# One place combination for split weights, and three changes of order, in a two-layer hybrid decoder trunk

## The chip, the cores and the metric

The kernel runs on one core of one Trainium2 chip. The metric is the device time of one execution in microseconds (us). Three runs of the kernel before took 598.81, 599.59 and 599.92 us, median 599.59. A difference of about 0.2% can be told from none.

## What is computed

Input and output are 256 tokens of width 1024 in float32. There are two layers, each a mixer and a feed-forward block, and a last norm:

```python
def rms_norm(x, g):
    return x * lax.rsqrt(jnp.mean(x * x, axis=-1, keepdims=True) + EPS) * g

def swiglu(h, w_gate, w_up, w_down):
    return (jax.nn.silu(h @ w_gate) * (h @ w_up)) @ w_down

# layer 0 mixer: RG-LRU (conv, gates, linear recurrence) beside stick-breaking attention
proj = h @ w_in;  out = concatenate([y_rg, y_sb]) @ w_out
# layer 1 mixer: S5 (diagonal complex state space model, gelu, GLU) beside block attention (MoBA)
proj = h @ w_in;  out = concatenate([y_s5, y_mb]) @ w_out

for layer in range(2):
    x = x + mixer(rms_norm(x, g_mix[layer]))
    x = x + swiglu(rms_norm(x, g_ffn[layer]), ...)
return rms_norm(x, final_norm)
```

The S5 branch has parameters of its own that come from few numbers: a step width exp(log_dt), from it a magnitude (tanh of xd/2 in the kernel) and a phase (sine of th), and from these powers and tables. They depend on no token.

## The kernel before

**Weights.** All dense weights lie in memory as 186 pieces of 128 x 1024 floats, in the order of their use. SyncE loads piece p into one of four buffers `raw`. ScalarE writes its rounded part `hi` (L109), VectorE the rest `lo` = raw - hi (L112). A product with float32 accuracy is then three TensorE matmuls: hi with the activations' high part, hi with their low part, lo with their high part (`dense` L152, `dense2` L163, the matmuls at L160 and L169; `proj_v` L352 with L368). A piece has eight blocks of 128 x 128 and so 24 such matmuls of 256 columns (in `proj_v` 12 of 512). `next_block` (L135) counts blocks. At the first block of piece p it has the piece p + 3 split and the piece p + 6 loaded; a load can land only where the piece four before it has been split.

**Places.** `split_tiles` (L102) takes the buffers of hi and lo out of one pool with five each, 1056 floats wide, and uses 1024 of them, from 0 or from 32 floats on, by a formula in p (L104). `half_line` reserves 16 floats between pools.

**Order.** TensorE and SyncE run in the order written. ScalarE, VectorE and GpSimd are put in order by the compiler's scheduler, from the written order and a model of times; `tc.issue_after(i)` makes the instructions of its block on i's own engine come behind i, and binds no other engine. Within an engine, order is fixed on the chip: an instruction that waits holds up all behind it.

**The norm.** x is split into xh and xl with the gain (`x_split` L219), unscaled by the token's 1/rms, which is multiplied in later. `x_square` (L210) squares x on ScalarE, two blocks at a time at the start, and GpSimd sums the squares (L215, L217). `rstd_a` (L237) sums over the partitions with TensorE (L241), takes a square root on ScalarE (L250; `preload_sqrt` at L202 loads its table early) and a chain of four small VectorE operations (L251 to L254). `rstd_b` (L257) spreads the result with TensorE (L260).

**Small operations in the background.** `s5_first` (L569) puts 38 VectorE operations of 128 x 16 on a list `bg`, the first part of the S5 parameters, down to xd (L606) and the clamped th (L612). `split_part` (L107) takes some from the list after each split: six up to piece 9, then two up to piece 40, then four. It is called before layer 0 begins (L1089).

**The start** (L1044 to L1089). x and pieces 0 and 1 are split in turns, then pieces 2 and 3, then all squares are taken behind piece 3's hi part. In `layer_ab` (L376), `softplus_setup` (L1022) does a Sigmoid on ScalarE, some 25 small GpSimd operations and a VectorE reciprocal (L1030) between them. The first `rstd_a` stands behind piece 4 in TensorE's order, `rstd_b` behind piece 5.

**S5 in the first feed-forward block.** `s5_prep` (L626) gives hooks that `ffn` (L273) calls. `early` (L801) comes after pair 0: `step0` (L646; Tanh L648, Sin L655 and L656, then small VectorE operations), `table` (L697; GpSimd products with `sq_phase` of VectorE between them), and GpSimd's larger work. All of it is told to issue after the norm's last sum (GpSimd) and after L254 (VectorE).

**The end of the second mixer** (`layer_cd` L815). `y_mm` (L896) computes a quarter of S5's output with 24 short matmuls, `y_gelu` (L905) takes it through four gelus on ScalarE. Quarters 0 and 1 come in the middle of `proj_v`, 2 and 3 behind it (L994, L995). Then come the four products of attention probabilities with v (`moba_av` L938; a copy to high part by ScalarE, L943, and low part by VectorE, L944), then four output columns of the projection that need only attention, then the S5 gate `dense(pg, yh, yl)`, which needs all quarters split (L1002, L1003).

Of the kernel before, what the change touches and what calls it, by code (L numbers as in the profile page):

```python
# [8 lines left out]
F32R = mybir.dt.float32r  # L9
AF = mybir.ActivationFunctionType  # L10
ALU = mybir.AluOpType
# [7 lines left out]
PI_F = 3.1415925  # L19
# [30 lines left out]
def trunk_kernel(  # L50
# [19 lines left out]
    def half_line(name, es=ctx, n=1):  # L70
        es.enter_context(tc.tile_pool(name="line_" + name, bufs=1)).tile([128, 16 * n], F32, name="line_" + name)
# [1 line left out]
    rawp = ctx.enter_context(tc.tile_pool(name="raw", bufs=LOAD_AHEAD - SPLIT_AHEAD + 1))  # L73
    half_line("a")
    wp = ctx.enter_context(tc.tile_pool(name="wp", bufs=SPLIT_AHEAD + 2))
    half_line("b", n=3)
    xp = ctx.enter_context(tc.tile_pool(name="xp", bufs=1))
    rp = ctx.enter_context(tc.tile_pool(name="rp", bufs=2))
    half_line("r")
# [5 lines left out]
    def nm(p):  # L85
        uid[0] += 1
        return f"{p}{uid[0]}"
# [13 lines left out]

    def split_tiles(p):  # L102
        if p not in hi:
            for d, n, o in ((hi, "hi", p // 6 + p % 5), (lo, "lo", p // 12 + p % 5 + 1)):  # L104
                d[p] = wp.tile([128, 1056], F32R, tag=n, name=nm(n))[:, 32 * (o % 2):32 * (o % 2) + 1024]

    def split_part(p, cs):  # L107
        split_tiles(p)
        last_hi[0] = S.activation(out=hi[p][:, cs], in_=raw[p][:, cs], func=AF.Copy)  # L109
        if pin:  # L110
            with tc.issue_after(pin[0].ins):
                i = V.tensor_sub(lo[p][:, cs], raw[p][:, cs], hi[p][:, cs])  # L112
        else:
            i = V.tensor_sub(lo[p][:, cs], raw[p][:, cs], hi[p][:, cs])
        with tc.issue_after(i.ins):
            for _ in range(min(BG if p > 40 else BG_AB if p < 10 else 2, len(bg))):
                bg.pop(0)()

    def split_half(p, c):
# [256 lines left out]
    def layer_ab():  # L376
# [128 lines left out]
        for j in range(2):  # L505
            ps = mmt()
            dense(ps[:, 0, :], xh, xl, ALL)
            if j == 0:
                y = rstd_a()
            dense(ps[:, 1, :], xh, xl, ALL)  # L510
            if j == 0:
                r = rstd_b(y)
                V.tensor_mul(xrp[:, 0, 3:T + 3], p2[0][:, 0, :], r)
                V.tensor_mul(xrp[:, 1, 3:T + 3], p2b, r)
                V.tensor_mul(xrp[:, 2:4, 3:T + 3], p2[1], bc(r, 2))
            V.tensor_mul(ti2[:, 2 * j:2 * j + 2, :], ps, bc(r, 2))
            conv(2 * j)
            conv(2 * j + 1)
# [50 lines left out]
    def s5_first():  # L569
# [8 lines left out]
        def ts(*a, **kw):  # L578
            ops.append(lambda: V.tensor_scalar(*a, **kw))
# [4 lines left out]
        def mul(*a):  # L584
            ops.append(lambda: V.tensor_mul(*a))
# [13 lines left out]
        for i in range(2):  # L599
# [3 lines left out]
            ts(out=g, in0=g, scalar1=127.0, scalar2=8388608.0, op0=ALU.add, op1=ALU.mult)  # L603
            ops.append(lambda: V.tensor_copy(out=gi, in_=g))
            mul(dt if i else p, p, gi.bitcast(F32))
        mul(xd, lr, dt)  # L606
        mul(th, li, dt)
        ts(out=k, in0=th, scalar1=1.0 / TWO_PI, scalar2=MAGIC, op0=ALU.mult, op1=ALU.add)
        ts(out=k, in0=k, scalar1=MAGIC, scalar2=None, op0=ALU.subtract)
        for c in (C1, C2, C3):  # L610
            stt(out=th, in0=k, scalar=-c, in1=th, op0=ALU.mult, op1=ALU.add)
        ts(out=th, in0=th, scalar1=PI_F, scalar2=-PI_F, op0=ALU.min, op1=ALU.max)  # L612
        bg.extend(ops)

    def s5_alloc():
# [10 lines left out]
    def s5_prep(es):  # L626
# [18 lines left out]

        def step0():  # L646
            xd, th, den, t = e16["xd"], e16["th"], e16["den"], t16("t")
            S.activation(out=t, in_=xd, func=AF.Tanh, scale=0.5)  # L648
            om, mag, em = t16("om"), t16("mag"), t16("em")
            V.tensor_scalar(out=om, in0=t, scalar1=-1.0, scalar2=1.0, op0=ALU.mult, op1=ALU.add)  # L650
# [164 lines left out]
    def layer_cd():  # L815
# [176 lines left out]
        pt[3] = moba_t(pr[3])  # L992
        ps1 = [mmt().rearrange("p a (b c) -> p (a b) c", c=64) for _ in range(2)]
        y_mm(ps1[0], 2)  # L994
        y_mm(ps1[1], 3)  # L995
        for h in range(4):
            moba_av(h, pt[h])
        y_gelu(ps1[0], 2)
        y_gelu(ps1[1], 3)
        for c in range(2):  # L1000
# [43 lines left out]
    with tc.manual_schedule(engines={mybir.EngineType.PE, mybir.EngineType.SP}):  # L1044
# [37 lines left out]
        x_split(4, 2, V_AB, lambda k: False)  # L1082
        split_half(1, 1)
        x_split(6, 2, V_AB, lambda k: False)
        split_to(3)
        with tc.issue_after(last_hi[0].ins):
            for k in range(0, 8, 2):
                x_square(k, 2)
        s5_first()  # L1089
        layer_ab()  # L1090
        s5_alloc()
        pes = ExitStack()
# [162 lines left out]
```

## Time and profile before

| | |
|---|---|
| median of 3 runs | 599.59 us |
| the profiled execution's own time | 598.55 us |
| its span, first to last instruction | 596.8 us |
| TensorE busy | 579.0 us, 97% |
| VectorE, ScalarE, GpSimd busy | 74%, 58%, 35% |
| mean granted TensorE clock | 0.994 |
| moved by DMA | 102.76 MB, mean 172 GB/s |

In the rows below, PE is TensorE, PEld its weight loads, DVE VectorE, ACT ScalarE, POOL GpSimd. L112 is line 112. Times are us from the span's start, unless ns. A timeline row gives start, duration, engine, line, operation, output<-inputs, shape and count, and in brackets the idle time before it with what ended it. Matmuls overlap and their ends are modelled, so the distance of two starts tells more than a duration.

### The profile page before, as it was taken

The numbers are of one execution on the slowest core, as the hardware profiler recorded it, in microseconds if no ns is written. First come the engines' busy times: TensorE is split into PE (matmuls) and PEld (weight loads), VectorE is DVE, ScalarE is ACT, GpSimd is POOL, SyncE is SP. The second block draws the span as 40 slices with busy tenths as digits, with TensorE's granted clock in tenths as the row PEclk, the third lists the DMA queues.
The fourth block names the chain that finished last, engine by engine and source line by source line (L and its number), as shares of the span: only waits on it lengthen the run. The fifth ranks groups of instructions, "written<-read, shape, count | busy, mean of one in ns | idle before, by whom it ended". The sixth has DMA issues, their size and how long they took to land.

```text
span 596.8 us, 11926 instructions
## 1 busy us (share of the span) xinstructions
PE 579.0 (97%) x4840; PEld 562.9 (94%) x4840; DVE 440.1 (74%) x636; ACT 346.2 (58%) x480; POOL 209.6 (35%) x203
## 2 busy tenths in 40 slices
PE   8899999999899999999999999999999999999994
PEld 7899889999799999999999998899999999999994
DVE  5798989896999986638966993688766665566632
ACT  6769996952345445464667268866645443445451
POOL 0810001538999999439920000013121110021131
PEclk9999999999999999999999999999999999999997
DMA  8755345653466676445544432264666666666601
GB/s 315 265 151 204 106 144 188 236 176 108 141 200 200 205 255 200 144 139 176 184 148 165 142 106 72 87 231 155 205 204 194 196 192 196 191 199 190 200 3 71
DMA packets 29319, 102.76 MB, mean 172 GB/s; under 512 B 3520, under 2 KB 3536, under 8 KB 29264
## 3 DMA queue, kind: packets, MB, share of 16 engines
q1 hardware_dynamic: 28080, 99.36, 51.0%
q10 hardware_dynamic: 864, 1.57, 0.7%
q0 software_dynamic: 320, 1.06, 0.5%
q8 instruction: 38, 0.62, 0.4%
q14 instruction: 17, 0.14, 0.1%
HBM read 100.93 MB, written 1.05 MB: 171 GB/s over the span
## 4 chain that ended last, share of the span: by engine, by line
PE 68%; DVE 13%; ACT 9%; issue 4%; POOL 3%; DMA 3%; SPq 0%; DVEq 0%; ACTq 0%; POOLq 0%
PE mm L160 59%; DVE lo L112 4%; PE mm L169 3%; ACT hi L109 2%; DMA raw<-wall 2%; ACT u L907 1%; DMA x<-xT 1%; PE ax L169 1%; PE ax L780 1%; POOL acc L217 1%; PE mm L903 1%; PE ax L852 1%; ACT s5tt L785 1%; POOL s5st L715 1%; POOL p_tmp L710 0%
## 5 line engine op out<-in xcount | busy, mean ns | idle before, releaser
L112 DVE TENSOR_TENSOR lo<-raw,hi 128x1024 fp32r<-128x1024 f32 x184 | 246.1, 1344 | 88.3 <-ACT hi L109 88.1
L109 ACT ACTIVATE hi<-raw 128x1024 fp32r<-128x1024 f32 (+1 forms) x188 | 195.3, 1048 | 166.5 <-PE mm L160 98.1
L160 PE MATMUL mm<-xh,hi 128*128 128x256 f32 x896 | 252.7, 282 | 0.8 <-ACT xh L943 0.7
L160 PE MATMUL mm<-xh,lo 128*128 128x256 f32 x896 | 248.8, 278 | 3.3 <-DVE lo L112 3.3
L160 PE MATMUL mm<-xl,hi 128*128 128x256 f32 x896 | 248.6, 277 | 0.2
L160 PEld LDWEIGHTS mm<-xh,lo 128*128 128x128 f32 x896 | 168.2, 188 | 4.4 <-DVE lo L112 4.3
L160 PEld LDWEIGHTS mm<-xh,hi 128*128 128x128 f32 x896 | 168.5, 188 | 1.8 <-ACT xh L943 1.2
L160 PEld LDWEIGHTS mm<-xl,hi 128*128 128x128 f32 x896 | 168.4, 188 | 0.9 <-DVE xl L944 0.8
L160 PE MATMUL mm<-hh,hi 128*128 128x256 f32 x312 | 86.2, 276 | 0.0
L160 PE MATMUL mm<-hh,lo 128*128 128x256 f32 x312 | 86.2, 276 | 0.0
L160 PE MATMUL mm<-hl,hi 128*128 128x256 f32 x312 | 86.2, 276 | 0.0
L215 POOL TENSOR_TENSOR acc<-sq 128x256 f32<-128x256 f32 x5 | 5.8, 1166 | 183.8 <-ACT sq L211 183.8
L304 POOL TENSOR_TENSOR t<-t,rstd 128x512 f32<-128x512 f32 x11 | 19.0, 1723 | 127.1 <-ACT t L303 127.1
L160 PEld LDWEIGHTS mm<-hh,lo 128*128 128x128 f32 x312 | 58.6, 188 | 0.0
L160 PEld LDWEIGHTS mm<-hh,hi 128*128 128x128 f32 x312 | 58.6, 188 | 0.0
L160 PEld LDWEIGHTS mm<-hl,hi 128*128 128x128 f32 x312 | 58.6, 188 | 0.0
L217 POOL TENSOR_TENSOR acc<-acc,sq 128x256 f32<-128x256 f32 x29 | 26.7, 920 | 22.9 <-ACT sq L211 21.6
L311 ACT ACTIVATE hh<-h 128x512 fp32r<-128x512 f32 x22 | 13.7, 621 | 26.0 <-DVE h L308 25.9
L326 DVE TENSOR_TENSOR x<-x,mm 128x256 f32<-128x256 f32 x32 | 13.2, 414 | 16.6 <-PE mm L160 14.6
L303 ACT ACTIVATE t<-t 128x512 f32<-128x512 f32 x22 | 13.7, 622 | 18.0 <-DVE t L302 17.6
L227 DVE SCALAR_TENSOR_TENSOR xl<-x,vec,xh 128x256 fp32r<-128x256 f32 x32 | 22.2, 709 | 2.4 <-ACT xh L225 2.3
L308 DVE TENSOR_TENSOR h<-mm,t 128x512 f32<-128x512 f32 x22 | 15.1, 687 | 8.9 <-PE mm L160 6.8
(333 smaller groups left out, 983.9 us busy)
## 6 DMA issues: line engine op xcount, KB each, us to landing
raw<-wall SPq DMA_DIRECT2D x184, 512.0 KB, 4.1
raw<-wall ACTq DMA_DIRECT2D x4, 256.0 KB, 5.4
x<-xT SPq DMA_DIRECT2D x4, 256.0 KB, 5.3
gw<-gates SPq DMA_DIRECT2D x1, 512.0 KB, 6.8
p_b<-bst POOLq DMA_DIRECT2D x1, 512.0 KB, 4.2
p_c<-cst POOLq DMA_DIRECT2D x1, 512.0 KB, 4.8
outT<-x SPq DMA_DIRECT2D x2, 256.0 KB, 2.5
outT<-x ACTq DMA_DIRECT2D x2, 256.0 KB, 2.5
```

The lines of the kernel that those rows point to most:

```text
L109: last_hi[0] = S.activation(out=hi[p][:, cs], in_=raw[p][:, cs], func=AF.Copy)
L112: i = V.tensor_sub(lo[p][:, cs], raw[p][:, cs], hi[p][:, cs])
L160: PE.matmul(ps, lhsT=w, rhs=a, start=(j == 0 and i == 0), stop=(j == n - 1 and i == 2))
L169: PE.matmul(pss[i], lhsT=w, rhs=a, start=(j == 0 and not begun), stop=(j == 2 and i not in [o for o, _ in order[n + 1:]]))
L217: acc_t[1] = G.tensor_add(out=acc_t[0], in0=acc_t[0], in1=sq[:, k, :])
L227: i = eng.scalar_tensor_tensor(out=xl[:, k, :], in0=x[:, k, :], scalar=gk, in1=xh[:, k, :], op0=ALU.mult, op1=ALU.subtract)
L303: S.activation(out=t, in_=t, func=AF.Silu)
L304: R.tensor_mul(t, t, bc(r[0], 2))
L308: V.tensor_mul(h, pu, t)
L311: S.activation(out=hh, in_=h, func=AF.Copy)
L326: V.tensor_add(x[:, k, :], x[:, k, :], pd)
L715: G.tensor_add(s1, a, b)
```

## The change

Five edits. hi and lo get a pool each, with buffers of 1024 floats and no offset; one of three half lines moves behind the second pool. `s5_first` is called behind the first `rstd_b` instead of before the layer, and six operations follow a split up to piece 13 instead of 9. Two of its 38 operations (xd and the clamp of th) move into `step0`. At the start, the squares are written between the splits. In the second mixer, the last quarter's `y_mm` is written behind the four `moba_av`.

```diff
-    half_line("b", n=3)
+    half_line("b", n=2)
+    wlp = ctx.enter_context(tc.tile_pool(name="wlp", bufs=SPLIT_AHEAD + 2))
+    half_line("x")
...
-            for d, n, o in ((hi, "hi", p // 6 + p % 5), (lo, "lo", p // 12 + p % 5 + 1)):
-                d[p] = wp.tile([128, 1056], F32R, tag=n, name=nm(n))[:, 32 * (o % 2):32 * (o % 2) + 1024]
+            hi[p] = wp.tile([128, 1024], F32R, tag="hi", name=nm("hi"))
+            lo[p] = wlp.tile([128, 1024], F32R, tag="lo", name=nm("lo"))
...
-            for _ in range(min(BG if p > 40 else BG_AB if p < 10 else 2, len(bg))):
+            for _ in range(min(BG if p > 40 else BG_AB if p < 14 else 2, len(bg))):
...
                 r = rstd_b(y)
+                s5_first()
...
-        mul(xd, lr, dt)
         mul(th, li, dt)
...
-        ts(out=th, in0=th, scalar1=PI_F, scalar2=-PI_F, op0=ALU.min, op1=ALU.max)
...
             xd, th, den, t = e16["xd"], e16["th"], e16["den"], t16("t")
+            V.tensor_mul(xd, lr, dt)
+            V.tensor_scalar(out=th, in0=th, scalar1=PI_F, scalar2=-PI_F, op0=ALU.min, op1=ALU.max)
             S.activation(out=t, in_=xd, func=AF.Tanh, scale=0.5)
...
         y_mm(ps1[0], 2)
-        y_mm(ps1[1], 3)
         for h in range(4):
             moba_av(h, pt[h])
+        y_mm(ps1[1], 3)
...
         x_split(6, 2, V_AB, lambda k: False)
+        x_square(0, 2)
+        split_to(2)
+        x_square(2, 2)
+        x_square(4, 2)
         split_to(3)
-        with tc.issue_after(last_hi[0].ins):
-            for k in range(0, 8, 2):
-                x_square(k, 2)
-        s5_first()
+        x_square(6, 2)
         layer_ab()
```

## Rows read from the trace of the kernel before

**Rows 1.** The page, part 1: busy us (share), instructions.

```profile
PE 579.0 (97%) x4840; PEld 562.9 (94%) x4840; DVE 440.1 (74%) x636; ACT 346.2 (58%) x480; POOL 209.6 (35%) x203
```

**Rows 2.** Waits of TensorE, whole span: us in total, times, longest.

```profile
PE mm L160 <- DVE lo L112: 3.3, 3, 2.1
PE ax L260 <- DVE rs L254: 2.4, 2, 1.7
...
PE ax L260 <- DVE p_ar L674: 1.0, 1, 1.0
```

**Rows 3.** Timeline of TensorE, 20 to 28 us.

```profile
20.07 0.28 PE L160 MATMUL mm<-xh,hi 128*128 128x256 f32 x1
...
21.72 0.28 PE L160 MATMUL mm<-xh,lo 128*128 128x256 f32 x1
...
22.67 0.28 PE L160 MATMUL mm<-xl,hi 128*128 128x256 f32 x1
23.53 0.39 PE L160 MATMUL mm<-xh,lo 128*128 128x256 f32 x1 [0.58 <-DVE lo L112]
...
24.23 0.28 PE L160 MATMUL mm<-xl,hi 128*128 128x256 f32 x1
...
26.04 0.28 PE L160 MATMUL mm<-xh,lo 128*128 128x256 f32 x1
27.98 0.49 PE L260 MATMUL ax<-con,rs 128*128 128x128 f32 x2 [1.67 <-DVE rs L254]
```

**Rows 4.** TensorE in 18 slow stretches: us, busy (matmuls), clock, DMA share, GB/s.

```profile
175.00:189.10 14.10, 14.10 (x121) 1.00 0.69 220
...
sum 78.90, PE 78.90; mean PE 4.38
```

**Rows 5.** TensorE in ten stretches of pieces 12 to 17, 36 to 41, ...

```profile
50.10:52.60 2.50, 2.50 (x23) 1.00 0.47 188
...
sum 111.70, PE 111.70; mean PE 11.17
```

**Rows 6.** Timelines of ScalarE, VectorE and GpSimd at the start.

```profile
13.21 1.06 ACT L109 ACTIVATE hi<-raw 128x1024 fp32r<-128x1024 f32 x1 [1.04 <-DMA raw<-wall]
14.18 2.18 ACT L211 ACTIVATE sq<-x 128x512 f32<-128x512 f32 x4
...
12.21 1.22 DVE L112 TENSOR_TENSOR lo<-raw,hi 128x1024 fp32r<-128x1024 f32 x1 [0.20 <-ACT hi L109]
...
22.14 0.18 DVE L1030 RECIPROCAL sp_b<-sp_b 128x4 f32<-128x4 f32 x1 [1.62 <-POOL sp_b L1029]
...
16.20 5.74 POOL L217 TENSOR_TENSOR acc<-acc,sq 128x256 f32<-128x256 f32 x6
```

**Rows 7.** Timelines of ScalarE and VectorE, 110 to 118 us.

```profile
110.66 1.28 ACT L648 ACT_TABLE_LOAD   x1
...
113.47 0.22 ACT L655 ACTIVATE p_sn<-e_th 128x16 f32<-128x16 f32 x1
...
115.71 1.28 ACT L250 ACT_TABLE_LOAD   x1
...
118.05 0.15 DVE L650 TENSOR_SCALAR p_om<-p_t 128x16 f32<-128x16 f32 x1
```

**Rows 8.** Busy time of all engines, 118 to 136 us.

```profile
118.00:136.00 18.00, 17.73 (x156) 17.76 (x157) 17.76 (x66) 10.19 (x13) 6.78 (x7) 1.00 0.52 172
```

**Rows 9.** TensorE during the S5 quarters 2 and 3.

```profile
367.00:372.30 5.30, 5.30 (x51) 1.00 0.30 92
```

**Rows 10.** Timelines of TensorE, ScalarE, VectorE, 374 to 382 us.

```profile
374.86 0.36 PE L160 MATMUL mm<-xh,hi 128*128 128x256 f32 x1
...
378.48 0.39 PE L160 MATMUL mm<-xl,hi 128*128 128x256 f32 x1
...
378.00 0.62 ACT L907 ACTIVATE u<-mm 32x256 f32<-32x256 f32 x1
...
380.88 1.28 DVE L1003 TENSOR_TENSOR syl<-u,syh 128x512 fp32r<-128x512 f32 x2
```

## The prediction

> **What bounds the kernel now.** I read the page first: TensorE is busy for 97% of the span [rows 1]. So a change pays only where TensorE waits, or where its matmuls come closer together. The list of what TensorE waited for puts first VectorE's low weight parts (L112) and the rstd chain (L254 and, beside it, L674) [rows 2]. The timeline of TensorE, read from start to start rather than by the idle times (a matmul's end is modelled), then gives the size of each wait. It also shows something the idle times hide: 16 dense matmuls start within 1.81 us between 24.23 and 26.04 us, 113.1 ns each, but 14 within 1.65 us between 20.07 and 21.72 us, 117.9 ns each [rows 3]. The granted clock is 1.00 in stretches of both kinds [rows 4, 5], so it is not the clock. Eighteen stretches with the slow spacing add up to 78.9 us [rows 4], about 670 matmuls, which cost 4.8 ns each: 3.2 us in all.
>
> **Part A, the places of the weights.** Count addresses in steps of 128 bytes (32 floats). A buffer of 1056 floats is 33 steps, so a buffer's number cancels the p % 5 in the old offset, if the pool hands its five buffers out in turn. What is left: the high part's place is odd or even by p // 6, the low part's by p // 12, and the four combinations take turns, six pieces each. After the change a buffer is 32 steps and the low pool begins 161 steps behind the high one: high even, low odd, for every piece. That is the combination of pieces 12 to 17, 36 to 41 and so on. In the stretches with this combination I find slow spacing only at 50.1 to 52.6 us and for some eight matmuls from 378.7 us; the ten stretches of it that I looked at, 111.7 us, hold just the first of these [rows 5]. That is 3.4 us of slow spacing in some 1,056 matmuls (120 us), 3%, against 78.9 us in all of the 4,320 matmuls (about 495 us), 16%. If all pieces behave like these, slow stretches shrink from 79 to about 14 us, and 65 us x 4.8 / 117.9 = 2.6 us are gained. Bounds: nothing (the spacing has another cause), and on the far side a combination that now holds the slow spacing everywhere, (495 - 79) us x 4.8 / 113.1 = 17.7 us lost. I take **-2.5 us**, near the first, since these rows are of the very combination.
>
> The rows show two spacings with no wait in them. The Trainium skill, SBUF — State Buffer, section "Who interferes with whom", says that TensorE has two independent read ports and that "PE and ACT never wait on anyone", from which I would conclude that a place in SBUF cannot matter; by that rule part A is worth 0 and the sum below is 2.5 us smaller. The trace neither shows nor excludes it, as no stretch compares two places with all else equal.
>
> **Part B, the start.** Before, ScalarE waits 1.04 us for a weight piece and then does four squares after it, from 14.18 us; GpSimd's sums run behind them until 21.94; only then comes the softplus step that VectorE waits 1.62 us for, with the low part of piece 5 queued behind it [rows 6]. TensorE loses 23.53 - 22.67 = 0.86, less a spacing: 0.75 us. VectorE, late by then, also works on the small S5 operations (0.15 us for one like them [rows 7], overlapping to about 0.1) between the steps of the rstd chain, and TensorE waits from 26.04 to 27.98 us, less 0.2 for the change of work: 1.74 us [rows 3]. Together 2.5 us.
>
> After the change the first squares stand before piece 2's copy, two more pairs in the 1.04 us gap, and the last behind piece 3's copy. GpSimd can begin at about 11.9, and seven sums at the 0.96 us of its row [rows 6] end near 18.6, 3 us earlier. The softplus step then waits only for its own Sigmoid (done at 19.2), and VectorE is free for piece 5's low part when the copy is there (20.2). The 36 remaining small operations come behind the splits of pieces 9 to 16, so the rstd chain runs undisturbed and ends at about 25.2, when TensorE is due. What they delay there: 36 x 0.1 = 3.6 us of VectorE between 31 and 53 us. Their cover is the lead of the low parts, 1.2 us for piece 9 (no small operation stands before it any more) and over 4 us for the following ones; without cover they would cost up to 3.6 us. No DMA moves, but loads follow the low part of four pieces before, so they come earlier too. The price: piece 2's copy is behind one square (2.18 / 4 = 0.55 us), its low part (12.21 to 13.43 us) ends as much later, and TensorE needs it at 13.48: 0.5 us lost, some of it made good because the wait for the sum at 22 us, a tenth or two, goes too. Gain between 1.0 and 2.5; I take **-2.1 us**, nearest to 2.5 less this price.
>
> **Part C, the first feed-forward layer.** Before, S5's Tanh and Sin run ahead of the rstd's square root, so ScalarE loads a table at 110.66, another before the sine at 113.47, and the square root's table again at 115.71, 1.28 us each [rows 7]. TensorE waits about 1.0 us for the chain [rows 2]. Two operations of 0.15 us now stand between the chain and Tanh and Sin, on VectorE and behind the chain; they force both behind the square root, whose table is already there. One load less, and this wait goes. But what is late next is S5 itself. The sines were ready before 114; now they need the root (about 114.9, as the load of 1.28 at 115.71 falls away), two loads and 0.6 us of work: 118.1 at best, with a weight copy between them 119.1. Before, their users started at 118.05 [rows 7]. VectorE is busy for 17.76 us of the 18 after that [rows 8], and the later waits of 2.1 and 0.7 us for L112 [rows 2] hang on this queue and its exchange with GpSimd. So TensorE's gain at 118 waits again at 152. Bounds: all three waits go (1.0 + 2.1 + 0.7 = -3.8 us), or S5 is a copy and a load later (+1.3 us). I take **-0.5 us**, near nothing.
>
> **Part D, the last S5 quarter.** Before, TensorE does 48 S5 matmuls in 5.3 us until 372.3, then sixteen attention products until 374.86 [rows 9, 10]. ScalarE's gelus of quarters 2 and 3 stand between its copies of the products, the last at 378.00, and the projection, begun at 374.86, has its eleventh matmul only at 378.48 [rows 10]. Unhindered that would be 0.2 + 9 x 0.113 = 1.2 us later than 374.86, at 376.1: 2.4 us lost. After the change the products end 2.6 us earlier (24 of 48 matmuls), and ScalarE has just quarter 2's four gelus, 2.5 us, to fit around four copies of 0.38 us before 374.86. The wait goes. The next in line: quarter 3's gelus now start at about 375.2 and end at 377.7, then come the two splits that ended at 382.16 before [rows 10], now about 379.7 or, with a weight piece between, 381; TensorE needs them at about 380.3. So between 1.0 and 2.4 us; I take **-2.2 us**.
>
> **Sum.** -2.5 - 2.1 - 0.5 - 2.2 = -7.3 us. The profiled execution took 598.55 us (span 596.8), so 591.25; it was 1.04 us below the median of the runs, 599.59, so I predict **592.3 us**.
>
> **Rivals.**
> - *The places don't matter* (A = 0): 594.8 us. For it: slow stretches begin after other matmuls or a wait and sometimes end within one combination. Against: only 3% under the kept combination. Chance 0.19.
> - *The compiler's order undoes B and D*: ScalarE's and VectorE's order is the scheduler's, so squares can still sit behind piece 3 and gelus before the copies; a third of B and D stays, 2.9 us less gain: 595.2, and with A = 0 597.7. Against: the products really do become ready 2.6 us earlier, whatever the order. Chance 0.11.
> - *S5's queue gets loose too* (C = -3.8): 589.0. For it: VectorE has 1.5 us without work before 115 now. Against: [rows 8]. Chance 0.08.
> - *Slower: the one combination holds the slow spacing.* In other combinations it lasted 14 us on end [rows 4]. If that is now so for all dense matmuls, +17.7 - 4.8 = +12.9 us: 612.5. It decides from where the slow share passes 79 / 495 + 4.8 / (495 x 4.8 / 113.1), 16% + 23% = 39% of the dense matmuls. For it: new distances between the two pools that no row shows. Against: [rows 5]. Chance 0.07.
>
> **Numbers.** The forecast itself has 0.55, 590 to 594.5 us. For 8 in 10 I add the first two rivals and the third: 589.0 to 597.2. A measurement of this kernel tells about 0.2% (1.2 us) from no change. Faster by more: forecast, first and third rival and most of the second, 0.89; within: a rest of the second, 0.04; slower: 0.07.
>
> **What would show it.** A: spacing near 113 ns in the stretches that now have 118, above all before 22 us, at 169 to 189 and 301 to 323 us. B: no wait of TensorE before the first L260, GpSimd's sums done by 19 us; wrong if a wait for L112 or L254 over 0.5 us remains. C: no square-root table load after Tanh; the wait before the second L260 gone, those for L112 near 152 us as long or longer. D: the projection after the attention products without wait for L943. The forecast fails if the spacing keeps its slow share, or if VectorE's small operations make TensorE wait for L112 at pieces 9 to 16.

## The result and the profile after

The kernel after takes 593.9 us (median of 4 runs, 593.54 to 594.85), before 599.75 us in the same comparison (598.81 to 600.43): a ratio of 0.9912, 95% interval 0.9895 to 0.9929, so 4.3 to 6.3 us faster. 592.3 us was forecast. Ratios, here and below, are taken over the runs of a kernel that lie within 1.5% of its fastest; only both_moved has others (3 of 12), and its profiled execution is one of them. The profiled execution took 593.54 us, its span is 591.8 us against 596.8, so 5.0 us are to be found. The page, part 1, of after:

```profile
PE 574.9 (97%) x4840; PEld 559.3 (95%) x4840; DVE 442.8 (75%) x636; ACT 344.8 (58%) x479; POOL 212.6 (36%) x203
```

TensorE is still the bound, with the same instructions; ScalarE has one less (a table load, 480 before [rows 1]). What TensorE waited for in after, us in total, times, longest:

```profile
PE mm L162 <- DVE lo L114: 3.7, 3, 2.5
PE ax L262 <- DVE rs L256: 1.5, 2, 0.8
...
PE ax L475 <- DVE z L467: 0.9, 1, 0.9
PE ax L465 <- DVE z L467: 0.6, 1, 0.6
...
PE ax L262 <- DVE e_xd L649: 0.3, 1, 0.3
```

Lines are two or three further down than before: L162 is the dense matmul (L160 before), L114 the low part (L112), L256 the end of the rstd chain (L254). Against [rows 2]: low parts cost 3.7 us instead of 3.3, the rstd chain 1.5 instead of 2.4, the S5 steps beside the second chain (now L649) 0.3 instead of 1.0. For z, a tile of the stick-breaking attention in the first layer, TensorE waited 1.5 us in after. In before it waited 0.4 us for z and 0.4 us for spl, another tile there:

```profile
PE ax L473 <- DVE z L465: 0.4, 1, 0.4
PE ax L463 <- DVE spl L492: 0.4, 1, 0.4
```

Followed piece by piece (start of a piece's first matmul, before and after), the lead grows and shrinks: 1.87 us at piece 6 (28.45 and 26.58), 2.05 at piece 16 (62.50, 60.45), **only 0.62 at piece 24** (94.36, 93.74), 1.42 at piece 32, 1.21 at piece 46 (160.34, 159.13), 2.24 at piece 110 (374.86, 372.62), 4.51 at piece 112 (382.94, 378.43), and so to the end. Most of what the changed first norm and the closer spacing had gained by 62 us had been given back by 94 us.

The closer spacing is there. I call a start slow that comes 115 to 125 ns after the one before (the others are at 113 ns). Of the some 4,270 matmuls of 256 columns with a weight piece 761 were slow in before and 187 are in after; above what 113.2 ns would take that is about 3.7 and 1.1 us. The counts shift by up to some 70 with how the edges of the band are taken (before between 744 and 761, after between 165 and 187), which changes none of the readings below. In after they stand in rows of at most nine, mostly right after TensorE did other work or waited.

### The profile page after: what moved, and what is told of

It reads as the page before. It is cut to its first block, busy times and chain, and to the rows that moved or that the text cites. A ratio compares the mean times of both kernels' runs of the same rounds, so it can differ in the third digit from the quotient of the medians.

```text
span 591.8 us, 11928 instructions
## 1 busy us (share of the span) xinstructions
PE 574.9 (97%) x4840; PEld 559.3 (95%) x4840; DVE 442.8 (75%) x636; ACT 344.8 (58%) x479; POOL 212.6 (36%) x203
## 4 chain that ended last, share of the span: by engine, by line
PE 69%; DVE 13%; ACT 8%; issue 3%; DMA 3%; POOL 2%; SPq 0%; DVEq 0%; ACTq 0%; POOLq 0%
PE mm L162 60%; DVE lo L114 5%; PE mm L171 3%; DMA raw<-wall 2%; ACT hi L111 2%; DMA x<-xT 1%; PE ax L783 1%; PE ax L171 1%; PE mm L906 1%; PE ax L855 1%; ACT u L910 1%; DVE xc L409 1%; ACT xh L227 1%; ACT s5tt L788 1%; POOL p_tmp L714 1%
## 5 line engine op out<-in xcount | busy, mean ns | idle before, releaser
L114 DVE TENSOR_TENSOR lo<-raw,hi 128x1024 fp32r<-128x1024 f32 x184 | 249.1, 1361 | 81.6 <-ACT hi L111 81.3
L162 PE MATMUL mm<-xh,hi 128*128 128x256 f32 x896 | 252.0, 281 | 0.0
L162 PE MATMUL mm<-xh,lo 128*128 128x256 f32 x896 | 248.4, 277 | 3.7 <-DVE lo L114 3.7
L162 PE MATMUL mm<-xl,hi 128*128 128x256 f32 x896 | 247.6, 276 | 0.0
L162 PEld LDWEIGHTS mm<-xh,lo 128*128 128x128 f32 x896 | 168.2, 188 | 4.9 <-DVE lo L114 4.4
L162 PEld LDWEIGHTS mm<-xh,hi 128*128 128x128 f32 x896 | 168.3, 188 | 0.6 <-issue 0.2
L162 PEld LDWEIGHTS mm<-xl,hi 128*128 128x128 f32 x896 | 168.4, 188 | 0.1
L162 PE MATMUL mm<-hh,hi 128*128 128x256 f32 x312 | 86.2, 276 | 0.0
L162 PE MATMUL mm<-hh,lo 128*128 128x256 f32 x312 | 86.1, 276 | 0.0
L162 PE MATMUL mm<-hl,hi 128*128 128x256 f32 x312 | 86.1, 276 | 0.0
L162 PEld LDWEIGHTS mm<-hl,hi 128*128 128x128 f32 x312 | 58.6, 188 | 0.0
L162 PEld LDWEIGHTS mm<-hh,hi 128*128 128x128 f32 x312 | 58.6, 188 | 0.0
L162 PEld LDWEIGHTS mm<-hh,lo 128*128 128x128 f32 x312 | 58.6, 188 | 0.0
L219 POOL TENSOR_TENSOR acc<-acc,sq 128x256 f32<-128x256 f32 x29 | 27.9, 963 | 23.6 <-ACT sq L213 22.4
```

The lines of the kernel that those rows point to most:

```text
L162: PE.matmul(ps, lhsT=w, rhs=a, start=(j == 0 and i == 0), stop=(j == n - 1 and i == 2))
L219: acc_t[1] = G.tensor_add(out=acc_t[0], in0=acc_t[0], in1=sq[:, k, :])
```

## The experiments

Ten kernels are after with one thing changed, one joins two of them, and one is before with part A alone. "Slow" counts slow starts; the last five columns are starts of pieces in the profiled execution (185 is the last one).

| kernel | median us | ratio to before (95%) | slow | piece 6 | 24 | 46 | 112 | 185 |
|---|---|---|---|---|---|---|---|---|
| before | 599.75 | 1 | 761 | 28.45 | 94.36 | 160.34 | 382.94 | 583.22 |
| after | 593.9 | 0.9912 (0.9895-0.9929) | 187 | 26.58 | 93.74 | 159.13 | 378.43 | 578.72 |
| places_undone | 594.85 | 0.9931 (0.9914-0.9947) | 601 | 27.08 | 94.12 | 159.46 | 379.15 | 579.54 |
| places_only | 597.2 | 0.9975 (0.9962-0.9987) | 213 | 29.20 | 95.01 | 160.91 | 383.86 | 584.21 |
| low_nearer | 597.21 | 0.9971 (0.9958-0.9984) | 1,063 | 26.75 | 94.60 | 161.76 | 382.82 | 583.02 |
| both_moved | 605.39 | 1.0066 (1.0031-1.0101) | 3,331 | 27.31 | 94.88 | 162.38 | 385.79 | 594.15 |
| rest_moved | 607.16 | 1.0145 (1.0124-1.0167) | 3,529 | 26.89 | 94.39 | 160.16 | 383.46 | 592.65 |
| squares_back | 594.54 | 0.9931 (0.9913-0.9949) | 210 | 26.91 | 94.36 | 159.70 | 379.06 | 579.30 |
| small_ops_back | 594.1 | 0.9928 (0.9905-0.995) | 218 | 28.65 | 93.97 | 160.66 | 379.06 | 579.40 |
| clamp_back | 594.02 | 0.9923 (0.9905-0.9942) | 197 | 26.91 | 93.86 | 160.26 | 378.77 | 579.07 |
| quarter_back | 596.85 | 0.9973 (0.9961-0.9984) | 194 | 26.80 | 93.78 | 160.32 | 381.15 | 581.52 |
| scores_first | 592.81 | 0.9894 (0.9876-0.9912) | 179 | 27.58 | 93.01 | 159.90 | 378.22 | 578.48 |
| own_tiles | 589.23 | 0.9843 (0.982-0.9865) | 183 | 26.75 | 94.01 | 155.70 | 374.03 | 574.34 |
| both | 587.42 | 0.9818 (0.9802-0.9834) | 189 | 26.84 | 92.31 | 153.87 | 372.17 | 572.47 |

The kernels were timed in groups, each beside before (598.1 to 598.8 us), so kernels of different groups are compared by their ratios. Two ratios with intervals of 0.0017 to either side differ safely only from about 0.0024 on (1.4 us); smaller parts are read from the starts, where a single execution has its own chances: piece 1, ahead of almost all that differs, already starts anywhere between 9.78 and 10.66 us, and places_only's profiled execution is its slowest of 12 (599.43 us).

### The places

places_undone (its edit is shown) takes part A out of after, places_only puts it alone into before, by the reverse edit; the order of instructions on every engine stays that of after and of before.

```diff
-    half_line("b", n=2)
-    wlp = ctx.enter_context(tc.tile_pool(name="wlp", bufs=SPLIT_AHEAD + 2))
-    half_line("x")
+    half_line("b", n=3)
...
-            hi[p] = wp.tile([128, 1024], F32R, tag="hi", name=nm("hi"))
-            lo[p] = wlp.tile([128, 1024], F32R, tag="lo", name=nm("lo"))
+            for d, n, o in ((hi, "hi", p // 6 + p % 5), (lo, "lo", p // 12 + p % 5 + 1)):
+                d[p] = wp.tile([128, 1056], F32R, tag=n, name=nm(n))[:, 32 * (o % 2):32 * (o % 2) + 1024]
```

> The kernel after with the old places alone (one pool, buffers of 1056 floats, the offset by piece number); the order on every engine is the one of after. Places theory: the closer spacing comes from the places. The slow starts (115 to 125 ns from one dense matmul to the next) rise from 187 to about 700, some 2.5 us of spacing, and as TensorE waits a little less in return where it waits for others anyway, the time rises by 1.5 to 2.5 us, to about 595.9. Rival (restarts): the slow spacing follows a restart of TensorE after other work or a wait, and there are fewer of those now; the count stays under 300 and the time within 0.4 us of after, 593.9.

> The kernel before with the new pools alone; the order on every engine is the one of before. Places theory: slow starts fall from 761 to about 190, 2.6 us of spacing, and 1.5 to 2.5 us of time are gained: about 597.7 where before has 599.7. Restart rival: the restarts of before are all still there, so the count stays near 760 and the time near 599.7.

Measured: 601 slow starts instead of 187, and 213 instead of 761. The places make the spacing; restarts alone do not. In time it is less than expected: 0.0019 of 599, 1.1 us, one way, which these intervals do not tell from nothing, and 1.5 us the other (interval 0.8 to 2.3). In places_undone the spacing above 113.2 ns grew by 1.7 us (from about 1.1 to 2.9), but the last piece starts only 0.82 us later. Part of the difference lies in the waits: between pieces 16 and 46 TensorE idles 0.45 us less in places_undone than in after. The rest is not explained.

The next three keep one combination for all pieces but another one. low_nearer puts the 128 bytes that lie between the two pools behind both; both_moved shifts both pools by 128 bytes and all behind them by 256; rest_moved leaves the pools and shifts all behind them by 128.

```diff
 low_nearer
-    half_line("b", n=2)
     wlp = ctx.enter_context(tc.tile_pool(name="wlp", bufs=SPLIT_AHEAD + 2))
-    half_line("x")
+    half_line("x", n=3)
 both_moved
-    half_line("a")
+    half_line("a", n=3)
-    half_line("x")
+    half_line("x", n=3)
 rest_moved
-    half_line("x")
+    half_line("x", n=3)
```

> The kernel after with the pool of the low parts 128 bytes nearer to that of the high parts (the 128 bytes go behind it, so that nothing else moves): 160 steps apart instead of 161, again one combination for every piece. In before this was the combination with the most slow starts, 395 of 1,108 (36%), where that of after had 36 of 1,042. Theory of this combination: about a third of all dense matmuls are slow, 1,300 to 1,700, 7 us of spacing instead of 1.15; the time rises by 4 to 6 us, to 598 to 600. Theory of any one combination (what costs is that the places change from piece to piece): under 300 slow starts, and 593.9 within 0.5 us.

> The kernel after with both pools, high and low parts, moved by 128 bytes (160 or 161 steps apart as before: 161), and all behind them by 256 bytes, so that the weights stand one step of 128 bytes differently against the activations and nothing else changes in distance or parity. In before the combination with both places odd had 135 slow starts of 1,078 (13%). Theory of the parities (each part's place against the activations): some 13%, 400 to 700 slow starts, 1.0 to 2.5 us above after. Theory of the distance (only the distance between a high part and its low part counts, 161 good, 160 bad): under 300 slow starts and 593.9 within 0.5 us.

> The kernel after with the pools of the weights where they are and everything behind them (the activations x, xh, xl and the later tiles) moved by 128 bytes. With both_moved the weights moved by 128 and the rest by 256 bytes, and 3,331 of some 4,270 starts were slow. Theory of the relation (what counts is how the weights stand to the activations): here that relation is the same one as in both_moved, so over 1,000 starts are slow and the time is 3 to 15 us above after. Theory of the own place (only where the weights themselves stand counts): the weights stand as in after, so under 300 starts are slow and the time is 593.9 within 0.5 us.

TensorE in one window of after, then of low_nearer, then of rest_moved (us, busy and matmuls, granted clock, DMA share, GB/s):

```profile
240.00:290.00 50.00, 49.57 (x437) 1.00 0.51 169
500.00:550.00 50.00, 50.00 (x444) 1.00 0.61 192
```

```profile
240.00:290.00 50.00, 49.58 (x422) 1.00 0.47 156
500.00:550.00 50.00, 50.00 (x443) 1.00 0.59 198
```

```profile
240.00:290.00 50.00, 49.57 (x428) 1.00 0.47 150
500.00:550.00 50.00, 50.00 (x423) 1.00 0.57 186
```

Between 500 and 550 us TensorE does nothing but the same matmuls with the granted clock at 1.00, and the window holds 444 of them in after, 423 in rest_moved: about 113 and 118 ns each. With the weights untouched, moving everything behind them by 128 bytes costs 14 us (0.0233 of 599). So not any one combination will do, and neither the weights' own places nor the distance of high and low part (161 steps in after and in rest_moved) decide it alone. low_nearer moves only the low parts, rest_moved only what lies behind the weights, and both change the spacing; that it is how the two stand to each other is the simplest reading, but no run moves them together by the same step, which would show it. Which of the tiles behind the weights counts was not tried either.

The table of before forecast these badly. The combination with 36% slow starts before gave 25% when kept (1,063); the one with 13% gave 78% in the profiled execution of both_moved. Slow spacing can last: in rest_moved some 1,485 slow starts follow one another from 419 us on; the longest row of before, with its changes of place, has some 120, that of after nine. And both_moved is not even the same from run to run: its 12 runs lie between 598.0 and 609.1 us, and the profiled one is the slowest, so its 78% stands for that execution alone. So the share of slow starts in a mix of places is no forecast for one place kept.

### The start

squares_back writes the squares behind piece 3 again; small_ops_back puts the small S5 operations behind the first pieces' splits again.

```diff
 squares_back
-        x_square(0, 2)
-        split_to(2)
-        x_square(2, 2)
-        x_square(4, 2)
         split_to(3)
-        x_square(6, 2)
+        with tc.issue_after(last_hi[0].ins):
+            for k in range(0, 8, 2):
+                x_square(k, 2)
 small_ops_back
-            for _ in range(min(BG if p > 40 else BG_AB if p < 14 else 2, len(bg))):
+            for _ in range(min(BG if p > 40 else BG_AB if p < 10 else 2, len(bg))):
...
-                s5_first()
...
+        s5_first()
         layer_ab()
```

> The kernel after with the squares of the first norm written behind piece 3's copy again; the S5 operations stay behind the first rstd. Swallowed theory: at the sixth piece after was 1.87 us ahead of before, at 94 us only 0.62, because TensorE then waits for the attention; so the squares' return costs 1.5 us or more at the sixth piece (26.6 becomes 28.1 or later) but only 0.4 to 1.0 at the end. Rival (gain kept): the end moves as the sixth piece does, by 1.5 to 2 us.

> The kernel after with the 36 small S5 operations behind the splits of the first pieces again (their call before the layer, six after a split up to piece 9); the squares stay in the gaps. Theory (B is the squares): the start is later by 0.2 to 0.6 us at most, for the operations between the steps of the rstd chain, and the end within 0.5 us of after. Rival (the small operations cost the attention its lead): VectorE is rid of them between 39 and 54 us, TensorE's waits for z near 83 and 88 us go, and the time falls by 0.6 to 1.2 us.

Both theories had the shares the wrong way round. Piece 6 starts at 26.91 in squares_back (0.33 later than in after) and at 28.65 in small_ops_back (2.07 later). Part of this is how each execution began: piece 1, ahead of what either edit moves, starts at 10.02 us in after, 9.80 in squares_back and 10.66 in small_ops_back. From piece 1 to piece 6 they take 16.56, 17.11 and 17.99 us (before 18.33). So the squares are worth about 0.5 us there and the small operations about 1.4. TensorE in squares_back, its waits from 20 to 28 us:

```profile
21.90 0.61 PE L243 MATMUL ax<-con,acc 128*128 128x1 f32 x4 [0.26 <-POOL acc L219]
...
23.43 0.39 PE L162 MATMUL mm<-xh,lo 128*128 128x256 f32 x1 [0.58 <-DVE lo L114]
...
26.44 0.71 PE L262 MATMUL ax<-con,rs 128*128 128x128 f32 x4 [0.23 <-DVE rs L256]
```

VectorE in small_ops_back, where all 128 x 16 operations are S5's (two of the five in a row are shown) and the first step of the rstd chain is the L253:

```profile
25.65 1.23 DVE L114 TENSOR_TENSOR lo<-raw,hi 128x1024 fp32r<-128x1024 f32 x1
26.79 0.17 DVE L587 TENSOR_TENSOR e_t<-e_t,e_r 128x16 f32<-128x16 f32 x1
...
27.20 0.17 DVE L587 TENSOR_TENSOR e_t<-e_t,e_r 128x16 f32<-128x16 f32 x1
27.29 0.16 DVE L253 RECIPROCAL rs<-rt 128x2 f32<-128x2 f32 x1
```

The square root of this execution is done at 26.0; the chain's first step waits in VectorE's queue until 27.29, behind a low part and five small operations, and then has others between its steps. TensorE's wait there is 2.17 us (1.67 in before, [rows 3]), though the squares run in their gaps. With the operations gone its waits are 0.26, 0.58 and 0.23 us in squares_back, 0.59 and 0.77 us in after. TensorE in after, 10 to 27 us:

```profile
13.88 0.39 PE L162 MATMUL mm<-xh,lo 128*128 128x256 f32 x1 [0.59 <-DVE lo L114]
...
26.12 0.71 PE L262 MATMUL ax<-con,rs 128*128 128x128 f32 x4 [0.77 <-DVE rs L256]
```

Of the 2.07 us only 0.23 are left at piece 24 (93.97 against 93.74). But this does not mean that the attention swallows any gain of the start. From piece 6 to piece 24 small_ops_back takes 65.32 us, after 67.16 and squares_back 67.45: with the small operations back, the scheduler also puts ScalarE's work near 60 us into the order of before again (next section). The kernels that keep this order with the early start, scores_first and both, take 65.43 and 65.47 us. At piece 32 small_ops_back is level with after (117.27 and 117.29 us). It loses 1.55 us by piece 46, where the granted clock fell to 0.50 from 156.7 to 160.1 us and in after did not, and has 0.97 of it back by piece 56, so its 0.68 us at the last piece are no measure of the small operations. squares_back, in the order of after, is 0.62 us behind at piece 24 and 0.58 at the last piece. So neither "kept" nor the numbers of "swallowed" came out: most of the start's gain was the small operations', and it went to an order that the same edit brought about.

### The attention

In after, ScalarE waits for the recurrence (L441, L442) before the attention's first Sigmoid (L485):

```profile
58.69 0.63 ACT L442 ACTIVATE yh<-xc 128x512 fp32r<-128x512 f32 x1 [1.35 <-DVE xc L441]
59.23 1.04 ACT L111 ACTIVATE hi<-raw 128x1024 fp32r<-128x1024 f32 x1
60.94 0.63 ACT L442 ACTIVATE yh<-xc 128x512 fp32r<-128x512 f32 x1 [0.67 <-DVE xc L441]
61.59 1.28 ACT L485 ACT_TABLE_LOAD   x1
62.88 1.49 ACT L485 ACTIVATE e<-z 128x1536 f32<-128x1536 f32 x1
```

In before the scheduler had the second of these copies behind the Sigmoid, and so it has in small_ops_back. ScalarE in before, then in small_ops_back:

```profile
63.21 1.49 ACT L483 ACTIVATE e<-z 128x1536 f32<-128x1536 f32 x1
64.61 0.61 ACT L440 ACTIVATE yh<-xc 128x512 fp32r<-128x512 f32 x1
```

```profile
62.87 1.50 ACT L485 ACTIVATE e<-z 128x1536 f32<-128x1536 f32 x1
64.26 0.62 ACT L442 ACTIVATE yh<-xc 128x512 fp32r<-128x512 f32 x1
```

scores_first holds it there; ScalarE's whole sequence of instructions in it is that of small_ops_back:

```diff
                 att_a(0)
+                with tc.issue_after(act["z"].ins), tc.issue_after(act["sig"].ins):
+                    rg_out(1)
                 att_b(0)
```

(`rg_out(1)` is the second half's product with the gate, its copy and its low part, taken out of `rg_chain2`.)

> The kernel after, with the second half of the recurrence's output (product, high and low part) held behind the first Sigmoid of the attention on ScalarE and behind the last score before it on VectorE; that is the order that the kernel before had there. Theory of the order: after lost 1.2 us between 73 and 94 us because ScalarE idles 1.35 and 0.67 us for the recurrence before the first Sigmoid, which starts at 62.88 us. Here the Sigmoid starts 1 to 2 us earlier, the waits of TensorE for z (0.6 + 0.9 us) go, and the time falls by 0.8 to 1.5 us, to about 592.8. Rival (the work as such): the stage from 60 to 94 us is bound by ScalarE's and VectorE's total work in any order; the waits come back for other tiles of the attention, and the time stays within 0.4 us of 593.9.

ScalarE in scores_first:

```profile
60.10 0.63 ACT L444 ACTIVATE yh<-xc 128x512 fp32r<-128x512 f32 x1 [1.03 <-DVE xc L443]
60.75 1.28 ACT L487 ACT_TABLE_LOAD   x1
62.05 1.49 ACT L487 ACTIVATE e<-z 128x1536 f32<-128x1536 f32 x1
```

This execution began a microsecond later (piece 6 at 27.58, a wait of 1.5 us for the rstd chain), so times are taken from piece 6: the Sigmoid comes at 34.47 instead of 36.30 us, and piece 24 at 65.43 instead of 67.16, **1.7 us sooner**. The waits for z and spl shrink from 1.5 to 0.8 us. So the order on ScalarE and VectorE cost after what it had gained, not the work as such. Of the 1.7 us 1.2 reach the last piece (550.90 us after piece 6, 552.14 in after), and the median fell by 1.1 us, as expected, though these two ratios alone are too near to each other to be told apart; the kernel both, below, repeats the gain.

On the way the lead was nearly gone once: from piece 44 to 46 this execution takes 10.73 us, after 9.08. TensorE in scores_first and then in after:

```profile
154.00:156.00 2.00, 0.34 (x2) 1.00 0.00 0
156.00:158.00 2.00, 2.00 (x12) 0.50 0.67 252
158.00:160.00 2.00, 2.00 (x13) 0.65 0.70 209
```

```profile
154.00:156.00 2.00, 0.04 (x1) 1.00 0.00 0
156.00:158.00 2.00, 1.49 (x13) 1.00 0.25 47
158.00:160.00 2.00, 2.00 (x20) 1.00 0.78 252
```

Both waited 2.46 us for a low part, until 155.66 and 156.51. Then the granted clock was 0.50, the lower of the two levels (1.2 GHz), for some three microseconds in the one and 1.00 in the other. A microsecond of the loss came back by piece 56 (27.20 us from 46 to 56, 28.19 in after), presumably because VectorE got ahead with the next low parts meanwhile.

### S5 in the first feed-forward block

clamp_back undoes part C, own_tiles goes at the waits behind it.

```diff
 clamp_back
+        mul(xd, lr, dt)
         mul(th, li, dt)
...
+        ts(out=th, in0=th, scalar1=PI_F, scalar2=-PI_F, op0=ALU.min, op1=ALU.max)
...
-            V.tensor_mul(xd, lr, dt)
-            V.tensor_scalar(out=th, in0=th, scalar1=PI_F, scalar2=-PI_F, op0=ALU.min, op1=ALU.max)
 own_tiles
-            sn, cs, u, w = t16("sn"), t16("cs"), t16("u"), t16("w")
+            u, w = t16("u"), t16("w")
+            cs, sn = t16("cs" + turn[0]), t16("sn" + turn[0])
+            turn.append(turn.pop(0))
...
-            V.scalar_tensor_tensor(out=sn, in0=cs, scalar=2.0, in1=sn, op0=ALU.mult, op1=ALU.mult)
-            V.tensor_sub(cs, w, u)
+            V.scalar_tensor_tensor(out=t16("sn" + turn[0]), in0=cs, scalar=2.0, in1=sn, op0=ALU.mult, op1=ALU.mult)
+            V.tensor_sub(t16("cs" + turn[0]), w, u)
```

(`turn` holds three suffixes in turn; `table` reads the pair written last.)

> The kernel after with xd and the clamp of th back among the small operations (part C undone). Theory: Tanh and Sin run ahead of the square root again, ScalarE loads its table once more, TensorE waits 1.0 to 1.3 us before the second rstd_b instead of 0.6, S5's tables start about 3 us earlier on GpSimd, and the two waits for low parts between 150 and 157 us (0.6 and 2.5 us) move with them but keep their sum within 0.6 us: the time is 0 to 0.8 us above after. Rival (S5's queue is what those waits hang on, and its lateness cost more than C gave): the sum of the two waits shrinks by over 1 us and the time is 0.5 to 1.5 us below after.

> The kernel after, with S5's squarings (a sine and cosine squared into the next on VectorE, while GpSimd still multiplies with the last ones) written in turn to three pairs of 128 x 16 tiles instead of one. Theory of the exchange: at 150 and 154 us the low parts that TensorE waits for stand behind a squaring that waits for GpSimd to have read its tile (VectorE idle 0.8 and 1.3 us). Without that the waits of 0.6 and 2.5 us go, and 2 to 3 us are gained, about 591 us. Rival (VectorE's work as such, or GpSimd's chain): the low parts are late for the sum of the work before them, other waits of the same size come back, and the time stays within 0.5 us of after.

In clamp_back TensorE's waits between 100 and 165 us are these two:

```profile
117.83 0.68 PE L262 MATMUL ax<-con,rs 128*128 128x128 f32 x4 [1.12 <-DVE p_ar L677]
...
153.31 0.38 PE L162 MATMUL mm<-xh,lo 128*128 128x256 f32 x1 [1.88 <-DVE lo L114]
```

The 1.12 us are back (0.32 in after), ScalarE loads the root's table at 115.27 again, and GpSimd's table begins at 135.23 instead of 139.14. At piece 32 the kernel has lost 0.80 us to after (4.57 us from piece 31, after 3.77). For that one wait of 1.88 us stands where after has 0.59 and 2.46, and although the clock fell to 0.50 behind it (154 to 156 us) 0.73 us are back by piece 56 (9.21 and 27.33 us, after 9.08 and 28.19). From piece 6 to the last one both take 552.1 us. So part C made S5 late by about what it gave: the rival's shorter waits, with the theory's unchanged time. As the clock fell in this execution and not in that of after, the sign of C's worth stays open.

own_tiles shows what these waits were. VectorE in after, around them:

```profile
143.33 0.20 DVE L695 SCALAR_TENSOR_TENSOR p_sn<-p_cs,p_sn 128x16 f32<-128x16 f32 x1 [0.82 <-POOL p_tmp L716]
...
146.38 0.25 DVE L695 SCALAR_TENSOR_TENSOR p_sn<-p_cs,p_sn 128x16 f32<-128x16 f32 x1 [0.97 <-POOL p_tmp L716]
...
148.94 0.36 DVE L695 SCALAR_TENSOR_TENSOR p_sn<-p_cs,p_sn 128x16 f32<-128x16 f32 x1 [0.79 <-POOL p_tmp L716]
...
151.50 1.11 DVE L314 TENSOR_TENSOR hl<-h,hh 128x512 fp32r<-128x512 f32 x1
153.94 0.57 DVE L695 SCALAR_TENSOR_TENSOR p_sn<-p_cs,p_sn 128x16 f32<-128x16 f32 x1 [1.33 <-POOL p_tmp L716]
...
155.24 1.21 DVE L114 TENSOR_TENSOR lo<-raw,hi 128x1024 fp32r<-128x1024 f32 x1
```

The high part for the L114 at 155.24 is done by 150.7. VectorE stands 1.33 us before a squaring of 16 columns that may not overwrite p_sn while GpSimd still reads it (L716), with the low part that TensorE needs queued behind. Four squarings in a row stand like this, 3.9 us in all. With a tile of its own for each turn, VectorE in own_tiles:

```profile
146.20 0.26 DVE L699 SCALAR_TENSOR_TENSOR p_sn<-p_cs,p_sn 128x16 f32<-128x16 f32 x1 [1.28 <-POOL p_tmp L720]
...
148.32 1.38 DVE L114 TENSOR_TENSOR lo<-raw,hi 128x1024 fp32r<-128x1024 f32 x1
...
150.49 1.43 DVE L114 TENSOR_TENSOR lo<-raw,hi 128x1024 fp32r<-128x1024 f32 x1
```

One such wait is left, early enough that TensorE does not wait behind it; the low part of 155.24 is begun at 150.49. The scheduler also moved squarings forward on VectorE and exchanged neighbouring products on GpSimd; ScalarE's order is that of after. Pieces 44 to 46 take 5.44 us instead of 9.08, no wait of TensorE remains from 140 to 165 us, and the time is 0.0069 of 599, 4.1 us, below after, more than the 2 to 3 expected: the two waits were 3.1 idle and 3.4 us from start to start, and the pieces after them gained another microsecond.

### The last quarter, and the two improvements together

```diff
 quarter_back
+        y_mm(ps1[1], 3)
         for h in range(4):
             moba_av(h, pt[h])
-        y_mm(ps1[1], 3)
```

> The kernel after with the last S5 quarter's 24 matmuls ahead of the attention products again (part D undone). Theory (part D as forecast): the projection waits for the fourth product's copy behind the gelus again, from piece 110 to piece 112 TensorE takes 8.0 us instead of 5.8, and the time rises by 2.0 to 2.4 us, to about 596. Rival: the wait is filled by part A's and C's other timing, and the time rises by under 1 us.

> The kernel of the squarings' own tiles together with that of the scores first. With scores_first alone TensorE was 1.7 us nearer to the sixth piece at 94 us, but the wait for the low parts near 153 us took it back. Theory: with that wait gone the 1.0 to 1.7 us reach the end, 587.5 to 588.2 us. Rival: the next wait takes them (the norm of the feed-forward block, or S5's chain on GpSimd), and the time is 589.2 within 0.4 us.

From piece 110 to 112 quarter_back takes 8.03 us, after 5.81: 2.2, as expected. TensorE in quarter_back, the projection's wait for the products' copies (the same stretch has none in after), and the S5 gate's first matmul:

```profile
376.28 0.38 PE L162 MATMUL mm<-xh,hi 128*128 128x256 f32 x1 [0.71 <-ACT xh L946]
...
381.15 0.28 PE L162 MATMUL mm<-syh,hi 128*128 128x256 f32 x1
```

In after that matmul starts at

```profile
378.43 0.28 PE L162 MATMUL mm<-syh,hi 128*128 128x256 f32 x1
```

The median is 0.0061 of 599 or 3.7 us above after (2.4 to 4.9 by the two intervals), which is more. The profiled execution took this median time, 596.85 us, and its last piece starts 2.80 us behind that of after: 2.2 from this wait, and 0.5 that it had lost before piece 110, behind a fall of the clock at 157 us. The rest of the 3.7 us stays open. The wait that D removes can cost the clock as well: in places_only, which has it too, the clock fell to 0.50 behind it and pieces 110 to 112 took 9.68 us. TensorE in places_only:

```profile
378.00:380.00 2.00, 2.00 (x13) 0.66 0.00 0
380.00:382.00 2.00, 2.00 (x11) 0.50 0.31 84
```

In the profiled executions of before and of quarter_back it stayed at 1.00 there (8.08 and 8.03 us).

both, with the edits of own_tiles and scores_first, takes 587.42 us, 0.9818 of before (0.9802 to 0.9834): the order's gain now reaches the end, as its theory said (piece 24 at 92.31, piece 46 at 153.87). It is the fastest kernel of this study, 0.0094 of 599, 5.6 us, faster than after. What TensorE still waits for in it:

```profile
PE ax L262 <- DVE rs L256: 2.0, 2, 1.2
...
PE mm L162 <- DVE lo L114: 0.6, 1, 0.6
```

## Why the prediction was right, and where not

The direction, the range (589.0 to 597.2) and the mechanisms of A and D held; the size was 1.6 us too optimistic. Between before and after the last piece gained 4.5 us, and 7.3 was forecast. Undone one by one, A costs 0.8, the squares of B 0.6 and C 0 to 0.35 us at the last piece, D 2.2 us at its place. The small operations of B come to 0.7, but with another order near 60 us and a fall of the clock in it, so these numbers make no clean sum.

- **A, -2.5.** The spacing gained 2.6 us, the size forecast, but the time 0.8 (last piece) to 1.5 us (places_only). The failing step is "65 us x 4.8 / 117.9 = 2.6 us are gained" as time: it took spacing gained just ahead of a wait as if it reached the end. Where TensorE waits for another engine anyway (z at 83 and 88 us, low parts at 151 and 156), part of it only makes the wait longer, 0.45 us against places_undone; where the rest goes is not shown. (The working's 4,320 dense matmuls are 4,272 of 256 columns and 96 wider ones, which changes nothing.) "Places don't matter" had 0.19 and fell. "Slower" had 0.07, which was thin: its price (17.7 us if all spacing were slow) was near, rest_moved has some 20 us of it and is 8.7 us (1.0145) slower than before, and it lay 128 bytes away. That the share under the old mix carried over was luck as much as reading; two of the three other places that were tried are slower than before.
- The rule of the Trainium skill quoted there (SBUF — State Buffer, "Who interferes with whom": TensorE and ScalarE never wait on anyone) does not cover this: the runs of places_undone, low_nearer and rest_moved, which differ from after in nothing but places, have 601, 1,063 and 3,529 slow starts against 187.
- **B, -2.1.** At piece 6 it was -1.87, near the forecast, but by other shares than the working has. There the small operations stand only between the chain's steps, "overlapping to about 0.1". In small_ops_back they also stand ahead of its first step, and are worth about 1.4 us; the squares are worth about 0.5. B's own sign of being wrong, a wait of over 0.5 us, came true: 0.59 us for a low part at 13.88 (the price that the working names) and 0.77 for the chain at 26.12. The chain did not end at 25.2 but at about 26.1. GpSimd's sums end at 20.2 us instead of 18.6, and ScalarE does a weight copy before it loads the root's table, so the root is done at 25.19 us, in before at 24.09. The step that failed for the end is the cover. "36 x 0.1 = 3.6 us of VectorE between 31 and 53 us" cost TensorE no wait for low parts there, but the working took the scheduler's order behind the start as given. Moving the small operations changed that order in the attention, which gave 1.4 us back by 94 us; with the old order held there (both) the gain lasts to the end.
- **C, -0.5.** Between 0 and -0.35, not told from nothing by times. S5's sines were done at 121.0 us, later than the 118.1 to 119.1 of the working. The working named the right place ("TensorE's gain at 118 waits again at 152") and the right queue. One rival took the end of both waits as a chance of 0.08 (589.0); own_tiles got to that time (589.23) by another edit, so the working had the right place for a gain that C did not bring.
- **D, -2.2.** 2.27 us in the profile, 2.2 by quarter_back.

## What to carry to other kernels

Before counting a gain, name the next stage whose work does not move with it, and compare the order of every engine before and after: here moving small operations out of the first 30 us changed the scheduler's order at 60 us, which took back most of what the start had gained. A tiny instruction that waits for another engine to finish reading costs what stands behind it in its queue, so three buffers in turn for a 16-column tile were worth more here (4.1 us) than any reordering. And when places in SBUF change the spacing of matmuls, measure the very layout: try it one 128-byte step to each side, and treat a fast one as fragile.

## What the runs showed of the hardware

- Matmuls of 256 columns with the granted clock at 1.00 start 113 or 118 to 119 ns apart, depending on where the weights and the tiles behind them lie: a move of 128 bytes turned 187 slow starts (after) into 3,529 (rest_moved). The slow spacing can last for some 1,485 matmuls in a row (rest_moved), and in the layout of after it ends by itself within nine.
- After a wait of 1.9 to 2.5 us near 150 to 157 us the granted clock was 0.50 for about three microseconds in some executions (scores_first, low_nearer, small_ops_back, clamp_back, quarter_back, both_moved) and stayed at 1.00 in others with the same wait (before, after, places_undone, places_only, squares_back, rest_moved). In places_only it fell at 378.6 us, behind a wait of 0.71 us. At the lower level the starts are 214 ns apart, and a drop cost up to 1.7 us, part of it made good where the next low parts were late anyway. What decides it these runs don't show; without the wait (own_tiles, both) it did not occur, and the runs of either kernel lie within 0.32 us.
